# One of two scaled rows on VectorE, one chain sum on VectorE, and a list schedule that also waits for operations that are nearly late

## The chip, the core and the metric

The kernel runs on one core of a Trainium2 chip. The metric is the device time of one execution in microseconds (us), the median of several. The core's engines work side by side, each through its own queue in order: TensorE (PE) multiplies matrices, VectorE (DVE), ScalarE (ACT) and GpSimd (POOL) work on tiles in SBUF and PSUM, SyncE (SP) issues transfers, and POOL's queue issues some too.

## The reference

A decoder of two layers on 512 tokens of width 1024, in fp32. Layer 0 has a pooling mixer, layer 1 a gated spatial unit (SGU). Each layer is followed by an MLP of width 4096 with a squared ReLU, and both halves of a layer are modulated: the norm's output is scaled and shifted, and the branch is added through a gate, by vectors that come from a conditioning vector and a weight matrix ("ada").

```python
def rmsnorm(x, g):
    xf = x.astype(jnp.float32)
    y = xf * lax.rsqrt(jnp.mean(xf * xf, axis=-1, keepdims=True) + RMS_EPS)
    return (y * g.astype(jnp.float32)).astype(x.dtype)

def modulate(h, shift, scale):
    return h * (1.0 + scale[:, None, :]) + shift[:, None, :]
...
    z = jax.nn.gelu(h @ w_in, approximate=False)
    u, v = jnp.split(z, 2, axis=-1)
    v = layernorm(v, ln_g, ln_b)
```

What matters here is the end of layer 0's MLP: its result is added to x, each row of x is scaled by the power -1/2 of its mean square, and the scaled rows, transposed and modulated, are what the SGU's first matmul multiplies.

## The kernel before, in words

Every fp32 product is made of three matmuls on rounded parts: an operand is split into a high part that ACT writes (wh for weights, hb or as for activations, op for sums of operands) and a low part that DVE writes (wl, and hb, as, op again). So each weight tile costs ACT one conversion and DVE one subtraction of 128x1024.

The MLPs save matmuls with a scheme of seven products in place of eight: in the first GEMM (the "s" units, function s_prep for their weights and s_run for their matmuls) a unit's weight is one of four blocks b(r, n) of a quad, or a chain of sums and differences of them. The blocks live in the tiles tr, yr and raw. Sums are made by DVE (V.tensor_tensor) or by a transfer that adds to what stands in SBUF (function add: G.dma_start with accum_op, on POOL's queue). A unit's matmuls go into a PSUM buffer po, which ACT and DVE empty into g. The second GEMM (the "p" units) makes 24 matmuls of 512 columns a unit into pm; its results go through y into the residual x by the epilogue function gated, which also takes the sum of squares (on ACT, with the square written to tmp), and DVE makes sums of it.

Function rms calls for one power on POOL (rr<-sums,mhalf, a tile of 128x1) per tile of 128 tokens. Function scaled_rows(hf) makes the two tiles xs of half hf: X(t) times its rr, both by ACT. Function normed then has PE transpose xs in 16 blocks of 128x128 into px, and ACT and DVE modulate and split them (tt, hb). Function ending0 calls it for the first half of the tokens at the end of layer 0's MLP, ahead of the last of the pm matmuls, so that these hide the modulation. The SGU's matmuls follow (po at L102).

The order of the work inside an MLP is made by a planner, class Plan. It records the engine calls of mlp (a proxy in place of each engine) and replays them in an order of its own, and all instructions that it replays show as line L130, all others that go through the same wrapper as L102. PE's order is fixed. For each operation the planner has a cost (method cost: for DVE columns / 960 + 0.065 us, for ACT columns / 1200 + 0.095, for transfers a rate by size) and a due time late, counted back from the fixed stream of PE. It runs through time: when an engine is free it takes from the operations that are ready the one that is due first. Function yields, for DVE and ACT, lets the engine stand idle in favour of an operation that becomes ready soon:

```python
            for j in soon[e]:
                slack = late[j] - cost[j][1]
                if j != i and eta[j] < end and slack < end and late[i] - cost[i][1] > max(slack, eta[j]) + cost[j][0] and fits(j):
                    return True
```

Here i is the operation that it would start now, end the time at which i would be done by its cost, eta[j] the time at which j becomes ready, and slack the latest time at which j may start. So the engine waits only for a j that would be late if i went first. LEAD (layer 0) and LEAD1 (layer 1) hold the times at which the engines begin in the plan.

Of the kernel before, what the change touches and what calls it, by code (L numbers as in the profile page):

```python
# [9 lines left out]
AF = mybir.ActivationFunctionType  # L10
ALU = mybir.AluOpType
PSUM = bass.MemoryType.PSUM
PE = mybir.EngineType.PE
# [54 lines left out]
SPILL = (5, 7)  # L68

COLUMNS = (0, 5, 8, 10, 12, 14, 16, 17, 19, 21, 23, 24, 26, 28, 30, 31, 33, 35, 37, 38, 41, 44, 47, 50)  # L70
LEAD = dict(SP=0.0, POOL=0.0, ACT=9.0, DVE=9.0, PE=13.0, fresh=7.0)
LEAD1 = dict(SP=0.0, POOL=0.0, ACT=9.0, DVE=9.0, PE=10.0, fresh=7.0)
PLAN = (True, True)
A_PARTS = ((0, 0, 1, 2, 7), (2, 2, 2, 3, 4))

# [1 line left out]
class Plan:  # L77
# [125 lines left out]
    def run(self, lead):  # L203
# [5 lines left out]
        cost = [self.cost(o[0], o[1], o[3], o[4], o[5]) for o in ops]  # L209
# [25 lines left out]
        t, at = lead["PE"], {}  # L235
# [4 lines left out]
        late = [0.0] * N  # L240
        for i in range(N - 1, -1, -1):
            x = min([late[j] - cost[j][1] for j in succs[i] if j > i], default=t + 20)
# [15 lines left out]
        def fits(i):  # L258
            need = {}
            for x in self.tiles[i]:  # L260
                if x in place and x not in opened:
                    t, k = place[x]
                    if t in self.fresh and now < lead["fresh"] or k != nxt[t] + need.get(t, 0) or held[t] + need.get(t, 0) >= caps[t]:
                        return False
                    need[t] = need.get(t, 0) + 1
            return True

        unstarted = [len(p) for p in self.preds]
        eta = [0.0] * N
        soon = {e: set() for e in ready}  # L270

        def yields(e, i):

            end = now + cost[i][0]
            for j in soon[e]:
                slack = late[j] - cost[j][1]
                if j != i and eta[j] < end and slack < end and late[i] - cost[i][1] > max(slack, eta[j]) + cost[j][0] and fits(j):
                    return True
            return False

        events, now, free, queue = [], 0.0, {e: lead[e] for e in ready}, 0.0
        for x in lead.values():
            heapq.heappush(events, (x, -1))
        for i in range(N):
            if any(ap.space == PSUM and ap.tensor.name not in place for ap in ops[i][3] + ops[i][4]):
                when[i] = lead["PE"]
# [82 lines left out]
def decoder_kernel(ctx: ExitStack, tc: tile.TileContext, xtok, vecs, fgrow, ada0, ada1, pool_w, w1s, w1, w1f, w1b, w2, w_v, w_u, w_o, wsT, lnp, bs, out):  # L369
# [70 lines left out]
    def X(t):  # L440
        return x_[t // 2][:, t % 2]
# [163 lines left out]
    with (  # L605
# [58 lines left out]
        def rms(t):  # L664
            V.tensor_scalar(v0[:, t : t + 1], ss[:, t : t + 1], RMS_EPS, None, ALU.add)
            G.tensor_tensor(r0[:, t : t + 1], v0[:, t : t + 1], mhalf[:, 0:1], ALU.pow)
# [338 lines left out]
    def mlp(i, first, extra, last, ending):  # L1005
# [3 lines left out]
        with (  # L1009
# [102 lines left out]
            def s_prep(u):  # L1112
                c, j, m = u

                def b(r, n):
                    return blk(c, j, r, n)

                def add(o, r, n):
                    G.dma_start(o, w1b[quad_at(c, j), r, n], accum_op=ALU.add)


                t = b(0, 0)
                if m in (5, 6):
                    V.tensor_tensor(t, t, b(*CHAIN[m]), ALU.add)
                if m == 5:
                    add(b(0, 1), 1, 1)
                if m == 4 and (c, j) == (3, 1):
                    V.tensor_tensor(t, t, b(*CHAIN[4]), ALU.add)
                wb = b(1, 1) if m == 3 else b(1, 0) if m == 2 else b(0, 1) if m == 7 else t
                w = split(wb)  # L1130
                if m == 6 and (c, j) != (3, 1):
                    add(t, *CHAIN[4])

                nxt = (c, j + 1) if j == 0 else (c + 1, 0)
                more = {1: [(c, j, 0, 1), (c, j, 1, 1)], 5: [(*nxt, 0, 0)], 6: [(c, j, 1, 0)], 3: [(*nxt, 0, 1)], 7: [(*nxt, 1, 1)]}.get(m, [])
                for at in more:
                    if at[0] < 4:
                        blk(*at)
                return w
# [238 lines left out]
    def rms(t):  # L1378
        return power(sums.pop(t)[0][:, 3:4], 1)

    def scaled_rows(hf):
        xs = []
        for r in range(2):
            t = w4.tile([P, D], F32, name="xs", tag="w4")
            A.activation(t, X(2 * hf + r), AF.Copy, scale=rms(2 * hf + r))
            xs.append(t)
        return xs

    def normed(hf, i, n, xs=None, ks=range(0, KD, 2)):

        xs = xs or scaled_rows(hf)
        c = slice(256 * hf, 256 * hf + 256)
        for k in ks:
            px = bank("px")
            for q in range(2):
                for r in range(2):
                    T.transpose(px[:, 256 * q + P * r : 256 * q + P * r + P], xs[r][:, P * (k + q) : P * (k + q) + P], ident)
            tt = h32[0][:, k : k + 2, c] if h32 else sm.tile([P, 2, 256], F32, name="tt", tag="tmp")
            for q in range(2):
                a, b = scl[i][n][:, k + q : k + q + 1], mod(i, c_sh(n, k + q))  # L1400
                if q:
                    A.activation(tt[:, q], px[:, 256:512], AF.Identity, bias=b, scale=a)
                else:
                    V.tensor_scalar(tt[:, q], px[:, 0:256], a, b, ALU.mult, ALU.add)
            parts(H(slice(k, k + 2), c), tt)
# [25 lines left out]

    def ending0():
        h_[0] = hparts()
        normed(0, 1, 0)

# [253 lines left out]
```

## Time and profile before

| | us |
|---|---|
| runs of the kernel | 813.9, 812.17, 813.31 |
| median | 813.31 |
| the profiled execution | 813.07 |
| its span | 811.4 |
| PE busy in it | 789.8 (97%) |
| DVE busy | 671.5 (83%) |
| ACT busy | 502.8 (62%) |
| POOL busy | 86.5 (11%) |

The profile is of one execution. Its span runs from the first instruction to the last, and 1.7 us lie around it. A timeline row has the start, the duration, the engine, the line, the operation with out<-in by the program's names, the number of instructions in the row, and in brackets how long the engine stood idle before it and what ended that. A row of the waits has the waiting engine and tile, the engine and tile that it waited for, the total in us, the number of times and the longest. Neighbouring instructions of an engine overlap somewhat: a DVE operation of 1.22 us is followed by the next one after 1.13 us, and a matmul of 0.38 us by the next one after 0.22 us.

### The profile page before, as it was taken

Reading aid. Unit: us, or ns where it says so; the run is one execution under the profiler, and the core shown is the slowest. Engines: PE = TensorE matmul, PEld = TensorE weight load, DVE = VectorE, ACT = ScalarE, POOL = GpSimd, SP = SyncE. Lnnn points to the kernel's source line nnn. Section 1 sums busy time; section 2 is a strip of 40 time slices with the busy share of each in tenths; the row PEclk is TensorE's granted clock in tenths of the full one; section 3 lists DMA queues with packets and bytes.
Section 4 is the critical chain, followed back from the end, with each engine's and each line's share of the span. In section 5 each row is a group of like instructions: output and inputs, shape, how many; then the busy total and the mean of one; then the engine's idle time right before and its main releaser. Section 6 shows DMA issues by size and latency. Waiting matters only on the chain.

```text
span 811.4 us, 12430 instructions
## 1 busy us (share of the span) xinstructions
PE 789.8 (97%) x4796; PEld 714.0 (88%) x4796; DVE 671.5 (83%) x872; ACT 502.8 (62%) x718; POOL 86.5 (11%) x110
## 2 busy tenths in 40 slices
PE   5999999999999999989999999999999999999996
PEld 5778899999988888878889889989999998888885
DVE  5989788999779997986798976847787877998796
ACT  5486677767766665766333226757767676666672
POOL 4000000000011121030020001000000011112100
PEclk9999999999999999999999999999999999999999
DMA  8989878886999999126755655575777499999802
GB/s 343 417 306 317 332 223 280 270 269 185 345 272 229 258 226 277 47 79 249 269 174 189 217 173 207 185 232 145 219 235 199 140 362 253 207 227 204 224 1 104
DMA packets 46955, 184.40 MB, mean 227 GB/s; under 512 B 5272, under 2 KB 5424, under 8 KB 42672
## 3 DMA queue, kind: packets, MB, share of 16 engines
q1 hardware_dynamic: 36432, 129.33, 43.3%
q0 software_dynamic: 10032, 51.92, 30.6%
q10 hardware_dynamic: 432, 2.36, 0.7%
q8 instruction: 38, 0.62, 0.3%
q14 instruction: 21, 0.17, 0.1%
HBM read 177.28 MB, written 6.30 MB: 226 GB/s over the span
## 4 chain that ended last, share of the span: by engine, by line
PE 90%; DVE 3%; ACT 3%; DMA 2%; POOL 1%; issue 1%; SPq 0%; POOLq 0%; ACTq 0%; DVEq 0%
PE pm L130 33%; PE po L130 31%; PE po L102 22%; PE px L102 1%; DVE wl L130 1%; DMA x<-in_xtok 1%; PE pq L102 1%; DMA yr<-in_w1b 1%; POOL rr L130 1%; DVE op L130 1%; ACT wh L130 1%; DVE tmp L130 0%; PE pt L102 0%; DVE x L130 0%; SPq L102 0%
## 5 line engine op out<-in xcount | busy, mean ns | idle before, releaser
L130 PE MATMUL pm<-wh,op 128*128 128x512 f32 x896 | 268.3, 381 | 0.0
L130 PEld LDWEIGHTS pm<-wh,op 128*128 128x128 f32 x896 | 170.3, 190 | 24.1
L130 PE MATMUL po<-hb,wh 128*128 128x256 f32 (+1 forms) x976 | 181.8, 291 | 0.6 <-DVE hb L130 0.6
L130 PE MATMUL pm<-wl,op 128*128 128x512 f32 x448 | 170.4, 380 | 0.0
L130 PEld LDWEIGHTS po<-hb,wh 128*128 128x128 f32 x976 | 152.6, 192 | 4.8 <-DVE hb L130 1.0
L130 PE MATMUL po<-hb,wl 128*128 128x256 f32 (+1 forms) x489 | 139.7, 291 | 0.4 <-ACT hb L130 0.4
L130 ACT ACTIVATE op<-g 128x1024 fp32r<-128x1024 f32 x56 | 59.2, 1059 | 59.9 <-PE pm L130 53.0
L130 PEld LDWEIGHTS pm<-wl,op 128*128 128x128 f32 x448 | 85.1, 190 | 11.9
L130 PEld LDWEIGHTS po<-hb,wl 128*128 128x128 f32 x489 | 92.5, 192 | 2.6 <-ACT hb L130 0.6
L130 DVE TENSOR_TENSOR op<-g,op 128x1024 fp32r<-128x1024 f32 x56 | 68.4, 1223 | 26.2 <-ACT op L130 26.1
L130 PE MATMUL po<-as,wh 128*128 128x256 f32 x528 | 89.1, 275 | 0.0
L130 PEld LDWEIGHTS po<-as,wh 128*128 128x128 f32 x528 | 80.3, 192 | 0.0
L130 DVE TENSOR_TENSOR wl<-bt,wh 128x1024 fp32r<-128x1024 f32 x64 | 77.4, 1220 | 3.5 <-ACT wh L130 3.5
L130 ACT ACTIVATE wh<-bt 128x1024 fp32r<-128x1024 f32 x64 | 67.2, 1053 | 17.2 <-PE pm L130 13.7
L130 PE MATMUL po<-as,wl 128*128 128x256 f32 x264 | 72.8, 276 | 0.9 <-ACT g L130 0.9
L130 DVE TENSOR_TENSOR wl<-tr,wh 128x1024 fp32r<-128x1024 f32 x44 | 53.7, 1224 | 23.6 <-ACT wh L130 23.5
L102 PE MATMUL po<-hb,wh 128*128 128x512 f32 x240 | 71.6, 380 | 0.0
L130 ACT ACTIVATE g<-g 128x512 f32<-128x512 f32 x97 | 59.9, 633 | 16.6 <-DVE g L130 15.2
L130 ACT ACTIVATE wh<-tr 128x1024 fp32r<-128x1024 f32 x44 | 46.4, 1058 | 32.5 <-DVE tr L130 22.5
L102 DVE SCALAR_TENSOR_TENSOR ada<-ada,cb 128x1024 f32<-128x1024 f32 x42 | 50.9, 1221 | 6.3 <-DMA ada<-in_ada 6.1
L130 PEld LDWEIGHTS po<-as,wl 128*128 128x128 f32 x264 | 50.7, 192 | 1.1 <-ACT g L130 1.1
L102 PEld LDWEIGHTS po<-hb,wh 128*128 128x128 f32 x240 | 45.2, 189 | 6.7 <-DVE hb L102 0.6
(210 smaller groups left out, 1256.9 us busy)
## 6 DMA issues: line engine op xcount, KB each, us to landing
ada<-in_ada SPq DMA_DIRECT2D x76, 512.0 KB, 4.6
bt<-in_w POOLq DMA_DIRECT2D x24, 1024.0 KB, 10.4
yr<-in_w1b SPq DMA_DIRECT2D x22, 512.0 KB, 5.7
b<-in_w SPq DMA_DIRECT2D x20, 512.0 KB, 8.5
bt<-in_w SPq DMA_DIRECT2D x16, 512.0 KB, 7.7
tr<-in_w1b SPq DMA_DIRECT2D x11, 512.0 KB, 4.9
raw<-in_w1b SPq DMA_DIRECT2D x11, 512.0 KB, 5.0
yr<-in_w1b POOLq DMA_DIRECT2D x11, 512.0 KB, 5.4
```

Source lines behind the costliest of these rows:

```text
L102: return f(*a, **kw)
L130: self.ops.append((name, attr, lambda: f(*a, **kw), out, ins, kw))
```

## The change

Four things change. The planner's numbers get an entry wait (1.5 us for layer 0, 3.0 for layer 1), and yields takes a j whose latest start lies up to wait behind the end of i, so an engine also stands idle for an operation that would not yet be late. The events of the plan's clock are named one by one, so that the new entry is none of them. In s_prep, the sum b(0, 1) + b(1, 1) of the first quad of each layer is made by DVE in place of the adding transfer on POOL's queue. And scaled_rows can have the second of its two rows made by DVE (V.tensor_scalar), which ending0 asks for.

```diff
-LEAD = dict(SP=0.0, POOL=0.0, ACT=9.0, DVE=9.0, PE=13.0, fresh=7.0)
-LEAD1 = dict(SP=0.0, POOL=0.0, ACT=9.0, DVE=9.0, PE=10.0, fresh=7.0)
+LEAD = dict(SP=0.0, POOL=0.0, ACT=9.0, DVE=9.0, PE=13.0, fresh=7.0, wait=1.5)
+LEAD1 = dict(SP=0.0, POOL=0.0, ACT=9.0, DVE=9.0, PE=10.0, fresh=7.0, wait=3.0)
...
-                if j != i and eta[j] < end and slack < end and late[i] - cost[i][1] > max(slack, eta[j]) + cost[j][0] and fits(j):
+                if j != i and eta[j] < end and slack < end + lead["wait"] and late[i] - cost[i][1] > max(slack, eta[j]) + cost[j][0] and fits(j):
...
-        for x in lead.values():
-            heapq.heappush(events, (x, -1))
+        for e in (*ready, "fresh"):
+            heapq.heappush(events, (lead[e], -1))
...
-                if m == 5:
+                if m == 5 and (c, j) == first_quad:
+                    V.tensor_tensor(b(0, 1), b(0, 1), b(1, 1), ALU.add)
+                elif m == 5:
                     add(b(0, 1), 1, 1)
...
-    def scaled_rows(hf):
+    def scaled_rows(hf, on_v=False):
...
-            A.activation(t, X(2 * hf + r), AF.Copy, scale=rms(2 * hf + r))
+            if on_v and r:
+                V.tensor_scalar(t, X(2 * hf + r), rms(2 * hf + r), None, ALU.mult)
+            else:
+                A.activation(t, X(2 * hf + r), AF.Copy, scale=rms(2 * hf + r))
...
-        normed(0, 1, 0)
+        normed(0, 1, 0, scaled_rows(0, True))
```

PE's instructions and their order stay as they were. DVE has two rows more of the chain sums and one of the scaled row, ACT one row less, POOL's queue two adding transfers less. The planner's new order shows first at the end of layer 0's MLP. On DVE, behind the last weight remainder (wl) and the last of y (tmp and x1 are the epilogue of token tiles 2 and 3), the difference is:

```order
 L130 TENSOR_TENSOR wl_1299<-bt_1157,wh_1298 128x1024
 L130 TENSOR_TENSOR y_1163<-y_1163 128x512 x2
+L130 TENSOR_SCALAR xs_1307<-x0_1248,rr_1308 128x1024
 L130 TENSOR_TENSOR tmp_1276<-y_1163,gb_1208 128x512
 L130 TENSOR_TENSOR tmp_1278<-y_1163,gb_1208 128x512
```

The row with the plus is new: the second scaled row stands between y and the epilogue, and waits there for the second power. On ACT at the same place (wh the high part of the last weight tile, tmp the squares of the epilogue, rr_1306 and rr_1308 the two powers):

```order
-L130 ACTIVATE wh_1298<-bt_1157 128x1024
 L130 ACTIVATE tmp_1251,sums_1252<-x0_1248 128x512
 L130 ACTIVATE tmp_1259,sums_1252<-x0_1248 128x512
+L130 ACTIVATE wh_1298<-bt_1157 128x1024
 L130 ACTIVATE xs_1305<-x0_1248,rr_1306 128x1024
-L130 ACTIVATE xs_1307<-x0_1248,rr_1308 128x1024
 L130 ACTIVATE tmp_1276,sums_1277<-x1_1265 128x512
```

The last two squares come ahead of the weight conversion, and one of the two xs is gone.

The second place is ACT at the start of layer 0's MLP (yr, raw and tr hold blocks of weights, g takes the products from po). Before:

```order
L130 ACTIVATE wh_1011<-yr_997 128x1024
L130 ACTIVATE g_980<-po_993 128x2x256
L130 ACTIVATE g_980<-g_980 128x2x256
L130 ACTIVATE wh_1013<-raw_1006 128x1024
L130 ACTIVATE g_999<-po_1000 128x512
```

Now:

```order
L130 ACTIVATE wh_1011<-yr_997 128x1024
L130 ACTIVATE g_980<-po_993 128x2x256
L130 ACTIVATE g_980<-g_980 128x2x256
L130 ACTIVATE g_999<-po_1000 128x512
L130 ACTIVATE wh_1013<-raw_1006 128x1024
```

The emptying of po_1000 and the weight conversion have changed places. The third place is ACT at the start of layer 1's MLP (h32 are the normed rows, hb their high part, wh a weight conversion):

```order
 L130 ACTIVATE hb_4349<-h32_4352 128x2x256
 L130 ACTIVATE h32_4352<-px_4777,mods1_90,scl11_94 128x256
+L130 ACTIVATE hb_4349<-h32_4352 128x2x256
 L130 ACTIVATE wh_4781<-raw_4780 128x1024
-L130 ACTIVATE hb_4349<-h32_4352 128x2x256
```

The last hb moves ahead of the weight conversion. On DVE, next to it (hb the low part, ada here a tile that holds a sum of h32):

```order
 L130 TENSOR_SCALAR h32_4352<-px_4777,scl11_94,mods1_90 128x256
-L130 TENSOR_TENSOR hb_4351<-h32_4352,hb_4349 128x2x256
+L130 TENSOR_TENSOR hb_4351<-h32_4352,hb_4349 128x2x256 x2
 L130 TENSOR_TENSOR ada_4804<-h32_4352 128x1024
-L130 TENSOR_TENSOR hb_4351<-h32_4352,hb_4349 128x2x256
 L130 TENSOR_TENSOR h32_4352<-h32_4352 128x4x256
```

Both low parts stand ahead of that sum now.

## The prediction, on record before the changed kernel ran

> **What bounds the kernel now.** I read the page's engine totals first, then the chain, then PE's waits, then timelines at each wait. TensorE (PE) is the bound:
>
> ```profile
> PE 789.8 (97%) x4796; PEld 714.0 (88%) x4796; DVE 671.5 (83%) x872; ACT 502.8 (62%) x718; POOL 86.5 (11%) x110
> ```
>
> PE's instructions and their order are the same in both kernels, so the change can only win time in which PE stands, or lose some. The waits by engine, PE's own:
>
> ```profile
> core 0 of [0], span 811.4 us
> ...
> PE px L130 <- ACT xs L130: 2.9, 2, 2.2
> PE po L130 <- ACT g L130: 0.9, 1, 0.9
> PE po L130 <- DVE hb L130: 0.6, 2, 0.3
> ...
> PE po L130 <- ACT hb L130: 0.4, 1, 0.4
> ```
>
> These four belong to three places, which I call A (end of layer 0's MLP, 352 us), B (start of layer 0's MLP, 123 us) and C (start of layer 1's MLP, 514 to 516 us). The rows left out lie at the program's start or inside the mixers (L102), which the planner doesn't order. The four add up to 4.8 us of waiting, and to somewhat more of lost time, as the places show.
>
> **Place A, the transition.** PE's timeline: the last down-projection matmuls (pm), the 16 transposes (px) of the scaled rows xs, 24 more pm held back to cover the norm, and the SGU's po.
>
> ```profile
> 352.36 0.38 PE L130 MATMUL pm<-wh,op 128*128 128x512 f32 x1
> 354.93 0.33 PE L130 MATMUL px<-ident,xs 128*128 128x128 f32 x1 [2.19 <-ACT xs L130]
> 355.97 2.33 PE L130 MATMUL px<-ident,xs 128*128 128x128 f32 x15 [0.71 <-ACT xs L130]
> 357.96 0.78 PE L130 MATMUL pm<-wh,op 128*128 128x512 f32 x1
> ...
> 364.31 0.38 PE L130 MATMUL pm<-wh,op 128*128 128x512 f32 x1
> 364.53 0.38 PE L102 MATMUL po<-wh,hb 128*128 128x512 f32 x1
> ```
>
> Dense matmuls of 512 columns follow each other after 0.22 us (364.31 to 364.53), so the first px could have started at 352.58. It started at 354.93, and the second at 355.97. Behind the stall the clock halves for one stretch (the windows view; the first column after the engines is the granted clock):
>
> ```profile
> 357.20:360.60 3.40, 3.40 (x12) 2.92 (x11) 3.05 (x5) 3.37 (x7) 0.00 (x0) 0.50 0.41 133
> ```
>
> That stretch holds 12 matmuls in place of 15 (3.40 / 0.22). Without a stall, 16 transposes take what they take elsewhere, with no slow matmul behind them:
>
> ```profile
> 508.24 1.91 PE L130 MATMUL px<-ident,xs 128*128 128x128 f32 x16
> ```
>
> So po would start at 352.58 + 1.91 + 24 x 0.22 = 359.77 and not at 364.53: **4.76 us** to win (1.91 includes the last one's latency, so the figure is on the low side).
>
> What PE waited for is the two xs on ACT, and these for the two powers rr on POOL:
>
> ```profile
> L130 POOL TENSOR_TENSOR rr<-sums,mhalf x2: 543/2872/5200, 348.5 to 353.7; 128x1 f32<-128x1 f32 x2
> ```
>
> ```profile
> 353.73 2.19 ACT L130 ACTIVATE xs<-x,rr 128x1024 f32<-128x1024 f32 x2 [5.75 <-POOL rr L130]
> ```
>
> The first power took 5.20 us, the second 0.54, on the same 128x1 tile. In the meantime DVE ran seven operations with two operands in SBUF without a gap:
>
> ```profile
> 348.20 0.33 DVE L130 TENSOR_SCALAR sums<-sums 128x1 f32<-128x1 f32 x2
> 348.44 1.22 DVE L130 TENSOR_TENSOR wl<-bt,wh 128x1024 fp32r<-128x1024 f32 x1
> 349.57 1.29 DVE L130 TENSOR_TENSOR y<-y 128x512 f32<-128x512 f32 x2
> ...
> 351.98 1.29 DVE L130 TENSOR_TENSOR x<-x,tmp 128x512 f32<-128x512 f32 x2
> ```
>
> The first power ended at 348.49 + 5.20 = 353.69, that is 0.42 us after this row's end (353.27). Two other powers of the trace, and what DVE ran beside the second of them:
>
> ```profile
> 488.42 0.56 POOL L102 TENSOR_TENSOR rr<-sums,mhalf 128x1 f32<-128x1 f32 x1 [59.98 <-DVE sums L102]
> ```
>
> ```profile
> 801.19 0.86 POOL L130 TENSOR_TENSOR rr<-sums,mhalf 128x1 f32<-128x1 f32 x1 [21.61 <-DVE sums L130]
> ```
>
> ```profile
> 800.97 0.68 DVE L130 TENSOR_TENSOR x<-x,cb 128x512 f32<-128x512 f32 x1
> ```
>
> The first, with no such work on DVE, took 0.56. The second took 0.86 and ended at 802.05, 0.40 us after that one two-operand operation (801.65). My reading: POOL was kept out until DVE's unbroken run of two-operand work ended. The Trainium skill (SBUF — State Buffer, section "SBUF: two separate sides") says that such a DVE operation and a GpSimd operation that reads SBUF exclude each other for one whole instruction, and that the blocked one goes on some 115 ns after DVE's end. By that letter the power would have come free behind the wl of 348.44, before 350; the trace has 353.69, so here the exclusion lasted over the run, or its length has another cause (the first rival).
>
> **What the change does at A.** The second xs goes to DVE, behind y and ahead of the four operations that followed (the pieces of the order stand with the change). DVE works in order, so it now stops at xs_1307 until both powers are done, and tmp and x1 queue behind it. Who waits for those: the norm of tiles 2 and 3, whose transposes come long after the first. On ACT, the squares come ahead of one weight conversion, and ACT has one xs less. Replayed from before's times: sums at 348.20, wl 348.44, y to 350.86; DVE stops; first power free at 350.86 + 0.42 = 351.28, second at 351.82. xs on ACT, half of the row's 2.19 with overlap (1.14): 351.31 to 352.45. xs on DVE by the nearest one-operand scaling of this shape:
>
> ```profile
> L102 DVE TENSOR_SCALAR v<-v,ag,rr 128x1024 f32<-128x1024 f32 x4 | 3.2, 811 | 0.6 <-POOL rr L102 0.4
> ```
>
> 0.81 us: 351.85 to 352.66, against 352.58 where PE wants it. That alone closes the gap to 0.1. And sums come earlier: an ada product that stood here moves ahead of DVE's idle times nearer 300 us,
>
> ```profile
> 319.89 1.22 DVE L130 SCALAR_TENSOR_TENSOR ada<-ada,cb 128x1024 f32<-128x1024 f32 x1
> ```
>
> which takes 1.13 us (1.22 less the overlap of neighbours) out of the stretch before sums. Cover: about 1 us. I take the whole 4.76; if the cover fails, each 0.1 us of lateness costs 0.1.
>
> **Place B.** ACT (first fence) and PE (second):
>
> ```profile
> 120.37 1.06 ACT L130 ACTIVATE wh<-yr 128x1024 fp32r<-128x1024 f32 x1 [0.64 <-DMA yr<-in_w1b]
> ...
> 122.49 1.04 ACT L130 ACTIVATE wh<-raw 128x1024 fp32r<-128x1024 f32 x1
> 123.43 0.58 ACT L130 ACTIVATE g<-po 128x512 f32<-128x512 f32 x1
> ```
>
> ```profile
> 122.66 0.28 PE L130 MATMUL po<-as,wl 128*128 128x256 f32 x1
> 122.77 0.39 PE L130 MATMUL po<-as,wh 128*128 128x256 f32 x2
> 124.06 0.38 PE L130 MATMUL po<-as,wl 128*128 128x256 f32 x1 [0.91 <-ACT g L130]
> ```
>
> PE's next matmul was due at 122.77 + 2 x 0.11 = 122.99 (0.11 from the first two rows) and started at 124.06: 1.07 lost. It needed the PSUM buffer that g<-po empties, and ACT did wh<-raw first, itself late since wh<-yr had waited 0.64 for the accumulating DMA. In the new order the two have changed places. Now g_999<-po_1000 starts where wh_1013 stood, by 122.49 at the latest, and by 121.9 with the DMA's 0.64 gone; its 0.58 ends between 122.5 and 123.1. **1.07 us** won (0.95 at least). Added for it: the chain sum on DVE, one two-operand operation of 128x1024 per layer, 1.22 us by the wl row above. It takes the place of one accumulating transfer on POOL's queue. DVE has 6.9 of 32 us free there, and 2.7 of 36 in the stage behind, where it has least room (the third column of times is DVE's):
>
> ```profile
> 92.00:124.00 32.00, 31.16 (x168) 27.77 (x167) 25.10 (x25) 25.73 (x39) 1.95 (x2) 1.00 0.75 244
> 124.00:160.00 36.00, 35.94 (x321) 35.94 (x322) 33.33 (x42) 25.11 (x36) 3.45 (x4) 1.00 0.86 281
> ```
>
> So 1.22 fits, and I cost it at nothing; in the stage behind it would still fit, and what doesn't fit would be PE's to wait, up to 1.2 in each layer.
>
> **Place C.** ACT, DVE, PE:
>
> ```profile
> 514.13 1.06 ACT L130 ACTIVATE wh<-raw 128x1024 fp32r<-128x1024 f32 x1
> 515.08 0.62 ACT L130 ACTIVATE hb<-h 128x512 fp32r<-128x512 f32 x1
> ```
>
> ```profile
> 514.42 1.22 DVE L130 TENSOR_TENSOR ada<-h 128x1024 f32<-128x1024 f32 x1
> 515.73 0.69 DVE L130 TENSOR_TENSOR hb<-h,hb 128x512 fp32r<-128x512 f32 x1
> ```
>
> ```profile
> 515.75 0.38 PE L130 MATMUL po<-hb,wl 128*128 128x256 f32 x1 [0.37 <-ACT hb L130]
> 516.48 0.49 PE L130 MATMUL po<-hb,wh 128*128 128x256 f32 x2 [0.35 <-DVE hb L130]
> ```
>
> The last hb stood behind wh on ACT, and its remainder behind ada on DVE. In the new order hb_4349 stands ahead of wh_4781 on ACT, and DVE's likewise has both hb_4351 ahead of ada_4804. hb moves from 515.08 to 514.13, the remainder from 515.73 to 514.78, PE's second start from 516.48 to 515.53: **0.95 us** won. What moves back is wh, by 0.6 us, and ada, by 0.7; nothing on PE waits for either in the waits above, and 0.7 is less than one conversion (1.06) of lead.
>
> **Elsewhere.** The waiting rule reorders DVE and ACT in both MLPs. Where PE is dense already it can win nothing. The end of the program:
>
> ```profile
> 803.81 0.69 DVE L130 TENSOR_TENSOR tmp<-pm,gb 128x512 f32<-128x512 f32 x1 [2.16 <-PE pm L130]
> ```
>
> DVE idles 2.16 us for PE's last pm; the new order puts two more epilogue operations (0.69 each) into that idle time: nothing, 0 to 0.6 at worst.
>
> **Sum.** The profiled execution took 813.07 us (span 811.4 and 1.7 around it), 0.24 under the median of 813.31. 813.07 - 4.76 - 1.07 - 0.95 = 806.29, so **806.3**. 0.2% is 1.6 us, about what a measurement can tell.
>
> **Rivals.**
> 1. *The 5.2 us belong to POOL, not to DVE's run.* Then the first power ends 5.2 after sums wherever DVE stands: with sums 1.13 earlier 352.56, the second 353.10, xs on DVE 353.9, and px 15 starts some 2.0 earlier than now; the halved clock (about 1.4) may go or stay. A gives 2.0 to 3.4, the total 807.6 to 809.0. For it: of the powers shown only this one is long. Against it: 0.56 at 488.42 after 59.98 us of idleness, and the 0.42 that matches the 0.40 of 801.19. The Trainium skill (GPSIMD Engine Reference, section "Instruction dispatch") has a first call of newly loaded code cost about 6 us, which would be such a case; the 488.42 row speaks against it. Chance 0.15.
> 2. *The gap moves to the start of the SGU.* Its first hb, its weights' remainders and their loads must follow po, now 4.76 us earlier. Replayed with before's durations they have 1 to 2 us of room, but the transfers' share of that is the least sure. If it is too short, 1 to 2.5 comes back: 807.3 to 808.8. Chance 0.12.
> 3. *Slower: DVE falls behind in layer 0's first GEMM.* Waiting leaves DVE idle on purpose, in the stage where 2.67 of 36 us are free (and 1.22 of new work stands ahead of it). From more than 2.67 per 36 us of waiting on, PE waits once a unit: at 0.25 in each of 35 units 8.75 us go, more than the 6.78 won: about 815. The order shows urgent work moved forward there, not late. Chance 0.06.
> 4. *It doesn't do what it says:* the planner's times aren't the chip's, and the three stalls stay in other places: 812 to 813.5. Chance 0.04.
>
> The forecast has 0.63. Range: 805.0 (0.28 if the first hb wait of C goes too, 0.2 for transposes that overlap their successors, 0.24 for run against run, and the rest of 1.3 for waits that I don't see) to 809.0 (rivals 1 and 2 in). Faster by over 0.2%: 0.63 + 0.15 + 0.12 = 0.90; within: 0.04; slower: 0.06.
>
> **What would show it.** Right: no PE wait for xs, clock 1.00 about 357, first power under 3 us and ended 0.4 after DVE's y; PE's wait for g and for ACT's hb gone; a remaining hb wait by DVE. Wrong: a power of 5 us with DVE idle (rival 1), a new wait of po at L102 behind the transition (rival 2), PE waits for wl in 124 to 160 (rival 3).

## The result and the profile after

| | before | changed |
|---|---|---|
| median, us | 813.31 (812.17 to 815.63, 7 runs) | 808.27 (807.09 to 811.49, 7 runs) |
| ratio | 1 | 0.9947, 95% interval 0.9929 to 0.9965 |
| the profiled execution, us | 813.07 (span 811.4) | 811.49 (span 809.8) |

The change makes the kernel faster by 0.35 to 0.71%, that is 2.8 to 5.8 us. The time lies in the range, and 2 us above the 806.3 that was named, which is below the fastest of the seven runs. The profiled execution of the changed kernel is the slowest of the seven, which turned out to matter.

PE's waits in the changed kernel, those at the start of the program and the shortest left out:

```profile
PE po L130 <- DVE g L130: 1.7, 4, 0.6
PE pm L130 <- DVE wl L130: 0.8, 1, 0.8
PE po L102 <- ACT hb L102: 0.5, 1, 0.5
PE po L130 <- DVE hb L130: 0.5, 2, 0.3
PE pm L130 <- DVE op L130: 0.5, 1, 0.5
```

The waits for xs, for ACT's g and for ACT's hb at L130 are gone, at A, B and C as foreseen (the wait for hb at L102, in the SGU, stood in the kernel before too). Three rows are new: g by DVE, wl and op.

**Place A.** PE's timeline over the transition, then the powers, DVE, and the clock of the stretch that had 0.50:

```profile
353.43 0.38 PE L130 MATMUL pm<-wh,op 128*128 128x512 f32 x1
353.64 1.91 PE L130 MATMUL px<-ident,xs 128*128 128x128 f32 x16
355.31 0.46 PE L130 MATMUL pm<-wh,op 128*128 128x512 f32 x1
...
360.57 0.38 PE L102 MATMUL po<-wh,hb 128*128 128x512 f32 x1
```

```profile
L130 POOL TENSOR_TENSOR rr<-sums,mhalf x2: 543/1666/2789, 347.8 to 350.5; 128x1 f32<-128x1 f32 x2
```

```profile
347.73 1.22 DVE L130 TENSOR_TENSOR wl<-bt,wh 128x1024 fp32r<-128x1024 f32 x1
348.86 1.29 DVE L130 TENSOR_TENSOR y<-y 128x512 f32<-128x512 f32 x2
351.12 0.75 DVE L130 TENSOR_SCALAR xs<-x,rr 128x1024 f32<-128x1024 f32 x1 [0.98 <-POOL rr L130]
```

```profile
357.20:360.60 3.40, 3.40 (x18) 2.97 (x17) 2.84 (x7) 3.30 (x7) 0.55 (x1) 1.00 0.98 377
```

From the last pm ahead of the transposes to the SGU's first po there were 12.17 us (352.36 to 364.53); now there are 7.14 (353.43 to 360.57). The first power ends at 350.56, 0.41 us after y (350.15). DVE idles 0.98 and then scales; xs is done at 351.87, 1.8 us before PE wants it.

**The new waits.** One of the four for g. ACT, DVE and PE about 150 us:

```profile
147.17 2.01 ACT L130 ACTIVATE wh<-tr 128x1024 fp32r<-128x1024 f32 x2 [2.14 <-DMA tr<-in_w1b]
```

```profile
148.26 2.36 DVE L130 TENSOR_TENSOR wl<-tr,wh 128x1024 fp32r<-128x1024 f32 x2 [2.66 <-ACT wh L130]
150.54 0.68 DVE L130 TENSOR_TENSOR g<-po,g 128x512 f32<-128x512 f32 x1
...
152.27 0.68 DVE L130 TENSOR_TENSOR g<-g,po 128x512 f32<-128x512 f32 x1
```

```profile
153.00 0.38 PE L130 MATMUL po<-hb,wl 128*128 128x256 f32 x1 [0.58 <-DVE g L130]
```

To be read from the top: ACT stood 2.14 us for the adding transfer tr, DVE 2.66 for ACT's wh, two remainders wl and then g queued behind that, and PE needed the PSUM buffer that g empties. DVE had been idle, so it isn't short of time there; it stood in front of one late transfer, in order. Added up over the nine places of the new waits (152, 172, 191, 229, 651, 660, 663 twice and 672 us), from one matmul's start to the next less the dense spacing, PE loses 4.8 us. Of the 6.9 us won at A, B and C (5.0, 1.07, 0.8) these leave 2.1, and the two profiled executions differ by 1.6.

### The profile page after: what moved, and what is told of

The parts are those of the page before. It is cut to its first block, busy times and chain, and to the rows that moved or that the text cites. A ratio compares the mean times of both kernels' runs of the same rounds, so it can differ in the third digit from the quotient of the medians.

```text
span 809.8 us, 12414 instructions
## 1 busy us (share of the span) xinstructions
PE 789.7 (98%) x4796; PEld 712.0 (88%) x4796; DVE 672.7 (83%) x875; ACT 502.1 (62%) x717; POOL 84.0 (10%) x108
## 4 chain that ended last, share of the span: by engine, by line
PE 69%; DMA 12%; DVE 10%; issue 4%; ACT 3%; SPq 0%; POOL 0%; POOLq 0%; DVEq 0%; ACTq 0%
PE pm L130 32%; PE po L102 17%; PE po L130 17%; DVE wl L130 3%; DMA b<-in_w 2%; DMA bt<-in_w 2%; DMA tr<-in_w1b 2%; DMA raw<-in_w 2%; DMA ada<-in_ada 2%; DVE ada L102 1%; PE px L102 1%; DMA x<-in_xtok 1%; ACT wh L130 1%; PE pq L102 1%; DVE g L130 1%
## 5 line engine op out<-in xcount | busy, mean ns | idle before, releaser
L130 PE MATMUL pm<-wh,op 128*128 128x512 f32 x896 | 268.2, 380 | 0.7 <-DVE op L130 0.5
L130 PEld LDWEIGHTS pm<-wh,op 128*128 128x128 f32 x896 | 169.3, 189 | 26.2 <-DVE op L130 1.9
L130 PE MATMUL po<-hb,wh 128*128 128x256 f32 (+1 forms) x976 | 182.0, 291 | 0.5 <-DVE hb L130 0.5
L130 PE MATMUL pm<-wl,op 128*128 128x512 f32 x448 | 169.9, 379 | 0.8 <-DVE wl L130 0.8
L130 PEld LDWEIGHTS po<-hb,wh 128*128 128x128 f32 x976 | 152.4, 192 | 4.7 <-DVE hb L130 0.8
L130 PE MATMUL po<-hb,wl 128*128 128x256 f32 (+1 forms) x489 | 139.8, 291 | 1.7 <-DVE g L130 1.7
L130 PEld LDWEIGHTS po<-hb,wl 128*128 128x128 f32 x489 | 92.4, 191 | 4.4 <-DVE g L130 2.5
L130 PEld LDWEIGHTS pm<-wl,op 128*128 128x128 f32 x448 | 84.7, 189 | 13.0 <-DVE wl L130 1.2
L130 ACT ACTIVATE op<-g 128x1024 fp32r<-128x1024 f32 x56 | 59.2, 1058 | 53.6 <-PE pm L130 45.7
L130 DVE TENSOR_TENSOR op<-g,op 128x1024 fp32r<-128x1024 f32 x56 | 68.5, 1223 | 25.0 <-ACT op L130 24.9
L130 PE MATMUL po<-as,wh 128*128 128x256 f32 x528 | 89.0, 275 | 0.0
L130 PEld LDWEIGHTS po<-as,wh 128*128 128x128 f32 x528 | 80.2, 192 | 0.0
L130 DVE TENSOR_TENSOR wl<-bt,wh 128x1024 fp32r<-128x1024 f32 x64 | 77.3, 1220 | 2.6 <-ACT wh L130 2.6
L130 ACT ACTIVATE wh<-bt 128x1024 fp32r<-128x1024 f32 x64 | 67.1, 1052 | 19.4 <-PE pm L130 15.0
L130 ACT ACTIVATE g<-g 128x512 f32<-128x512 f32 x97 | 59.6, 631 | 28.0 <-DVE g L130 26.8
L130 DVE TENSOR_TENSOR wl<-tr,wh 128x1024 fp32r<-128x1024 f32 x44 | 53.4, 1223 | 26.5 <-ACT wh L130 26.5
L130 PE MATMUL po<-as,wl 128*128 128x256 f32 x264 | 72.6, 275 | 0.0
L102 PE MATMUL po<-hb,wh 128*128 128x512 f32 x240 | 71.6, 380 | 0.0
L130 ACT ACTIVATE wh<-tr 128x1024 fp32r<-128x1024 f32 x44 | 46.0, 1056 | 18.6 <-DVE tr L130 9.4
L102 DVE SCALAR_TENSOR_TENSOR ada<-ada,cb 128x1024 f32<-128x1024 f32 x42 | 50.8, 1220 | 5.9 <-DMA ada<-in_ada 5.8
L102 PEld LDWEIGHTS po<-hb,wh 128*128 128x128 f32 x240 | 45.1, 189 | 6.8 <-DVE hb L102 0.6
L130 PEld LDWEIGHTS po<-as,wl 128*128 128x128 f32 x264 | 50.7, 192 | 0.0
```

The costliest lines, as they stand in the source:

```text
L102: return f(*a, **kw)
L130: self.ops.append((name, attr, lambda: f(*a, **kw), out, ins, kw))
```

## The experiments

The theory after the first look: A, B and C are won whole, and what is missing goes to transfers that land late, because the new plan orders them otherwise; how late differs from one execution to the next. The rivals: the new order itself makes those waits; DVE's added work and idling make them; the length of the power is POOL's own.

**The changed kernel once more (e1_again).** No edit.

> The changed kernel once more, unaltered, for a second profile. In its first profile PE lost about 4.8 us at nine new waits (four of po for DVE's g, three of pm for op, one for wl, one for ACT's wh), each behind a load that landed late. Theory: these come from transfers that collide, so their sum differs from one execution to the next; the second profile loses 1 to 4 us in such waits, and the median is 807 to 809.5. Rival (the order alone makes them): the same nine waits, 4.8 us within 0.5. Place A, B and C stay won in either case: no wait for xs or for ACT's g.

Measured: 807.8 us (805.67 to 810.49), ratio 0.9946 (0.9926 to 0.9966). The profiled execution took 805.67, the fastest of its six, and its PE waits from 18 us on are these:

```profile
PE po L102 <- ACT hb L102: 0.5, 1, 0.5
PE po L130 <- DVE hb L130: 0.5, 2, 0.3
PE po L102 <- DVE hb L102: 0.3, 1, 0.3
```

None of the nine. Program and order are the same, so the order alone doesn't make them. The adding transfers tr of 125 to 195 us in the kernel before, in the changed one's first profile and in this one (size, median us to landing):

```profile
tr<-in_w1b POOLq DMA_DIRECT2D x3, 512.0 KB, 5.6
```

```profile
tr<-in_w1b POOLq DMA_DIRECT2D x3, 512.0 KB, 7.8
```

```profile
tr<-in_w1b POOLq DMA_DIRECT2D x3, 512.0 KB, 7.3
```

The one of 138 us took 8.7 in the first profile and 7.3 in the second. In both, tr lands later than before, and in the execution of 811.49 it crosses the point where PE waits. The two yr on SP's queue right behind that tr took 8.0 and 7.8 in the one and 6.6 and 6.5 in the other, while POOL needed 0.85 us to issue tr in both: all the loads of that stretch were slower, not the adding transfer alone. Likewise the two b of 646 and 643 us took 13.2 and 10.3 (median of the two). The expectation of 1 to 4 us in a second profile was still too high: it was 0.

**Scaled row and chain sums, no waiting rule (e2_rows_chain).**

```diff
-LEAD = dict(..., wait=1.5)
-LEAD1 = dict(..., wait=3.0)
+LEAD = dict(..., wait=0.0)
+LEAD1 = dict(..., wait=0.0)
```

> The changed kernel with both entries wait at 0: only the scaled row and the chain sums are on DVE. Theory: place A is won whole (5.0 us), place B by the 0.64 us that ACT no longer waits for the adding transfer, place C stays lost (1.15), and none of the new waits of 124 to 230 and 645 to 672 us comes, since the loads keep their order: 807.7 (807 to 808.5), with less spread than the changed kernel. Rival (the new waits come from DVE's added work): the waits of po for DVE's g stay, 1.5 us or more in the profile, 809 to 811.

Measured: 809.88 us (808.48 to 811.77), ratio 0.9969 (0.9956 to 0.9982). A is won, C is lost as foreseen, but behind B waits stand that I had not expected (1.2 and 1.5 us lost at 126 and 143). ACT, then PE, at the first:

```profile
125.31 1.06 ACT L130 ACTIVATE wh<-tr 128x1024 fp32r<-128x1024 f32 x1 [2.43 <-DMA tr<-in_w1b]
126.28 0.58 ACT L130 ACTIVATE g<-po 128x512 f32<-128x512 f32 x1
```

```profile
126.91 0.38 PE L130 MATMUL po<-as,wl 128*128 128x256 f32 x1 [1.03 <-ACT g L130]
```

So ACT no longer waits for yr, and waits for tr a little later, again with g queued behind. The rival's number fits better than mine, but its mechanism doesn't: these two waits are ACT's, for a transfer (only a third one, 0.5 at 193 us, is for DVE's g). The three tr from 125 to 195 us took 7.6 us here (median), with no waiting rule.

**The scaled row alone (e3_rows_alone).**

```diff
+            if on_v and r:
+                V.tensor_scalar(t, X(2 * hf + r), rms(2 * hf + r), None, ALU.mult)
...
+        normed(0, 1, 0, scaled_rows(0, True))
```

> The kernel before with one edit, the second scaled row on DVE; no waiting rule, no chain sum on DVE. Theory: the first power ends 0.4 us after the end of DVE's y and PE doesn't wait for xs: 5.0 us won, B and C as before (1.07 and 1.15 lost): 808.3 (807.5 to 809). Rival 1 of the prediction (the 5.2 us belong to POOL): already against the changed kernel's profile, 2.79; here it would be 5.2 again and 811 or more. Second rival (A needs the squares that the waiting rule moves forward): a px wait of 0.1 to 1.3 us, 808.5 to 809.6.

Measured: 808.49 us (808.07 to 809.3), ratio 0.9950 (0.9937 to 0.9964), no wait for xs, power 2.79. One edit of the four gives the measured gain. The SGU's start gives some of A back here (0.15, 0.24 and 0.77 lost at 361 to 371 us, where the kernel before lost 0.38), for example:

```profile
372.31 0.48 PE L102 MATMUL po<-wh,hb 128*128 128x512 f32 x1 [0.72 <-DVE hb L102]
```

That is rival 2 of the prediction at a small price; with the waiting rule in layer 0 it is back to 0.38. C is lost here (1.15) as foreseen, and 0.97 for DVE's g at 652 us; at B nothing is lost, though the order there is that of before. Against e2_rows_chain only the chain sums are left out: the median is 1.4 us lower (the two intervals just overlap), and tr took 5.8.

**The waiting rule alone (e4_wait_alone).**

```diff
-    normed(0, 1, 0, scaled_rows(0, True))
+    normed(0, 1, 0)
...
-    if m == 5 and (c, j) == first_quad:
+    if m == 5 and False:
```

> The kernel before with the waiting rule alone (1.5 and 3.0); both scaled rows on ACT, chain sums by transfers. Theory: A stays (the first power runs until DVE's run of two-operand work ends, 4 us or more, px waits 2 to 3 us), B and C are won (1.07 and about 0.8), and the new waits cost 1 to 5 us: 812 to 816, no faster than before. Rival (the rule is worth its 1.9 and costs nothing by itself): 811.4.

Measured: 811.02 us (809.54 to 813.45), ratio 0.9988 (0.9974 to 1.0001): no difference that shows. But A went otherwise than expected. The powers, and DVE beside them:

```profile
L130 POOL TENSOR_TENSOR rr<-sums,mhalf x2: 934/2604/4273, 347.6 to 348.5; 128x1 f32<-128x1 f32 x2
```

```profile
347.40 0.68 DVE L130 TENSOR_TENSOR y<-y 128x512 f32<-128x512 f32 x1
347.99 0.21 DVE L130 TENSOR_SCALAR sums<-sums 128x1 f32<-128x1 f32 x1
...
351.06 1.28 DVE L130 TENSOR_TENSOR x<-x,tmp 128x512 f32<-128x512 f32 x2
```

The rule put one y between the two sums. The first power ended with that y (348.08 + 0.41 = 348.49), the second took 4.27 and ended 0.43 after x (352.34). So PE loses only 0.4 at px (the wait of 0.3 for the second xs), and the transition takes 7.65 us. The gain is lost elsewhere:

```profile
PE po L130 <- DVE g L130: 2.0, 2, 1.5
PE po L102 <- DVE wl L102: 1.1, 1, 1.1
PE po L102 <- ACT wh L102: 0.8, 1, 0.8
```

**Light ada transfers in the changed kernel (e5_light_after) and in the kernel before (e6_light_before).**

```diff
+        if attr == "dma_start" and out[0].tensor.name.startswith("ada"):
+            self.ops.append((name, attr, lambda: f(a[0][:, 0:64], a[1][:, 0:64], **kw), out, ins, kw))
...
```

and their products read the 64 columns fifteen times. The replay line is L138 in these.

> The changed kernel with the planner's order untouched, but the 42 or so ada transfers inside the two MLPs bring 64 columns in place of 1024 (their products read these over and over, so the modulation vectors of the later parts are not the reference's). About 16 MB fewer are moved. Theory: the new waits of PE come from transfers that land late because ada's share the 16 DMA engines with them; the adding transfer tr lands within 6.5 us instead of 6.8 to 8.7, PE waits for DVE's g nowhere in layer 0, and the median is 805 to 806.3 with runs within 2 us. Rival (the order itself, or DVE idling on purpose, makes them): 807 to 808.5 as in the changed kernel, and waits for g in the profile.

> The kernel before with the same ada transfers cut to 64 columns (the same part of the result left out), the control for the kernel above. Theory: before has few waits behind late transfers, at most place B (1.07) and nothing in the other stages: 811 to 812.3, so that changed against before is worth 6 us or more when ada's traffic is gone. Rival (the traffic costs both kernels alike): 2 us less as well, 810.

Measured: 807.49 (806.99 to 809.07), ratio 0.9940 (0.9924 to 0.9957), and 811.89 (809.88 to 814.93), ratio 0.9996 (0.9983 to 1.001). PE's waits in the changed kernel with light transfers, and its tr:

```profile
PE pm L138 <- DVE wl L138: 0.8, 1, 0.8
PE po L138 <- DVE g L138: 0.6, 1, 0.6
```

```profile
tr<-in_w1b POOLq DMA_DIRECT2D x3, 512.0 KB, 5.6
```

From 125 us on tr lands as in the kernel before, and no new wait is left in layer 0; the one for g stands at 648 us, those for op and wl at 657 to 670, in layer 1 (2.7 us lost), with ada's transfers as light there. So in this profile, with ada's transfers light, tr isn't late. That this is what freed PE in layer 0 isn't shown, since e1_again lost nothing there with full transfers. The median didn't fall for it, and the difference to the control, 4.4 us of medians, is no larger than with full transfers. My theory's number (805 to 806.3) failed.

The control shows something of A. Its waits for xs are those of the kernel before (2.34 and 0.92 us lost at px, 2.35 and 0.92 there), but the granted clock stayed whole behind them:

```profile
351.60 0.38 PE L138 MATMUL pm<-wh,op 128*128 128x512 f32 x1
354.15 0.33 PE L138 MATMUL px<-ident,xs 128*128 128x128 f32 x1 [2.18 <-ACT xs L138]
...
362.07 0.38 PE L102 MATMUL po<-wh,hb 128*128 128x512 f32 x1
```

```profile
356.40:359.80 3.40, 3.40 (x20) 3.05 (x19) 3.05 (x5) 3.37 (x7) 0.00 (x0) 1.00 0.51 135
```

The transition took 10.47 us, 3.3 more than in the changed kernel. Of the 12.17 in the kernel before, 1.7 belong to the halved clock, which didn't follow on the same stall here.

**Without the chain sums (e7_rows_wait), and with the rule in layer 1 alone, without them (e8_rows_w1).**

```diff
-                if m == 5 and (c, j) == first_quad:
-                    V.tensor_tensor(b(0, 1), b(0, 1), b(1, 1), ALU.add)
-                elif m == 5:
+                if m == 5:
...
-LEAD = dict(..., wait=1.5)
+LEAD = dict(..., wait=0.0)
```

(the last two lines in e8_rows_w1 only).

> The changed kernel without the chain sums on DVE (adding transfers as before): scaled row and waiting rule. Theory: the sum on DVE is worth nothing once g stands ahead of the weight conversion at B; 807 to 808.5, B without a wait of PE. Rival (the sum costs, as the scaled row alone at 808.49 against scaled row with sums at 809.88 suggests): 806 to 806.9. Second rival (B's gain comes from the sum): 808.5 to 809 with PE waiting at 122 us.

> Scaled row on DVE and the waiting rule in layer 1 alone (0 and 3.0), no chain sums on DVE. Theory: layer 0 keeps the order and the landings of the scaled row alone (808.49, tr within 6 us), place C is won (0.8), and layer 1's loads at 645 to 672 us may land late (0 to 2.8): 807.5 to 809. Rival (layer 0's rule is what wins, at the SGU's start 0.8 and at B): 808.5 to 809.5. Were it under 807, layer 0's rule would cost more than it wins.

Measured: 809.48 (807.69 to 811.89), ratio 0.9962 (0.9947 to 0.9976), and 809.1 (807.58 to 810.84), ratio 0.9956 (0.9937 to 0.9974). Neither differs from the changed kernel by more than the intervals. In the first, B has no wait though yr comes by transfer, as the order of g and wh would have it; PE loses 1.1 at 209 and 1.0 at 650 us for g. Its tr of 138 us has the neighbours that it has in the changed kernel and landed in 5.8 us, the next two in 7.5 and 7.6. In the second B is lost again (1.2).

**A stop of DVE without the scaling (e9_stop).** The kernel before, both xs on ACT:

```diff
+            q = rms(2 * hf + r)
+            if on_v and r:
+                q, p = sm.tile([P, 1], F32, name="rq", tag="rq"), q
+                V.tensor_scalar(q, p, 1.0, None, ALU.mult)
+            A.activation(t, X(2 * hf + r), AF.Copy, scale=q)
...
+        normed(0, 1, 0, scaled_rows(0, True))
```

> The kernel before, both scaled rows still on ACT, but the second one's power goes through a DVE copy of 128x1 behind y, so DVE stops there for the powers as it does in the changed kernel, and no 128x1024 work moves. Theory (the power runs until DVE's unbroken run of two-operand work ends): first power about 2.8 us in place of 5.2, xs end one after the other about 353.5, PE stands about 0.9 us in place of 3.2 and its clock stays whole: 3 to 4 us won, 808.5 to 810. Rival (what helps is the scaling moved off ACT, and the power's length is its own): power 5.2, 811.5 to 813.

Measured: 808.07 (807.42 to 810.1), ratio 0.9952 (0.9938 to 0.9966). DVE, POOL and PE:

```profile
348.85 1.28 DVE L130 TENSOR_TENSOR y<-y 128x512 f32<-128x512 f32 x2
351.12 0.15 DVE L130 TENSOR_SCALAR rq<-rr 128x1 f32<-128x1 f32 x1 [0.98 <-POOL rr L130]
```

```profile
L130 POOL TENSOR_TENSOR rr<-sums,mhalf x2: 544/1668/2792, 347.8 to 350.5; 128x1 f32<-128x1 f32 x2
```

```profile
352.83 1.86 PE L130 MATMUL px<-ident,xs 128*128 128x128 f32 x15 [0.70 <-ACT xs L130]
```

This decides the cause at A. An operation of 0.15 us, which only makes DVE stand for 0.98 us, shortens the power from 5.20 to 2.79 us as the scaled row does, and gives a gain as large as the change's (0.9952 against 0.9947). The second scaling on ACT leaves a wait of 0.70 at px, which moving it saves: the transition takes 8.06 us here and 7.14 in the changed kernel.

**A plan with slower transfers (e10_slow_plan), and the rule in layer 0 alone (e11_w0).**

```diff
-            return (5.05 * mb, 3.6 + 4.8 * mb) if kw.get("accum_op") else (2.7 * mb, 0.9 + 5.2 * mb)
+            return (5.9 * mb, 4.6 + 5.6 * mb) if kw.get("accum_op") else (3.1 * mb, 1.5 + 6.0 * mb)
```

and, in the second, wait=0.0 in LEAD1.

> The changed kernel, and the planner takes transfers to be slower: 3.1 us per MB and 1.5 + 6.0 per MB to landing (2.7, 0.9 + 5.2 before), adding ones 5.9 and 4.6 + 5.6 (5.05, 3.6 + 4.8). Theory: PE's new waits come from transfers that land later than the plan has them, so a plan with later landings loads urgent weights ahead of ada and loses less: 805.7 to 807.2, fewer and shorter waits for g, op and wl in the profile. Rival (the stretch at 640 to 665 us is short of bandwidth whatever the order): 807.5 to 808.5 with waits at 648 to 672.

> The changed kernel with the waiting rule in layer 0 alone (1.5 and 0). Theory: C is lost again (0.8), the waits of 657 to 672 us (up to 1.9 in two of three profiles of this order) go, what is left in layer 0 stays: 807 to 808.8, no difference that these runs can tell from the changed kernel. Rival (layer 1's rule costs more than it wins): under 806.8; second rival (it wins): over 809.

Measured: 841.01 (840.23 to 842.05), ratio 1.0355 (1.0339 to 1.0372), and 807.82 (806.8 to 809.96), ratio 0.9947 (0.993 to 0.9964). The slower plan is 28 us slower than the kernel before and 33 slower than the changed one. The longest piece of the chain before the transition, and PE's longest waits:

```profile
358.64 3.81 DMA gb<-gain
```

```profile
PE px L130 <- ACT xs L130: 9.4, 1, 9.4
PE pm L130 <- DVE wl L130: 7.5, 4, 2.3
PE pm L130 <- ACT wh L130: 6.3, 3, 2.1
```

It also moves the transfer of the gain vector (gb) and the ada products to the end of the MLP, where the epilogue waits for them. So a plan that takes transfers to be slower isn't a safer one here, against the theory. The rule in layer 0 alone is no different from the changed kernel; its profile has waits at 190 to 228 us (1.6) and C's (1.15) but none at 650 to 672.

**The rule only where it moves no transfer (e12_parts).**

```diff
-... slack < end + lead["wait"] and ...
+... slack < end + (lead["wait"] if lead["PE"] > 11 and now > 150 or lead["PE"] < 11 and now < 40 else 0.0) and ...
```

without the chain sums.

> The scaled row on DVE, and the waiting rule only where it moves no transfer: in layer 0 from the plan's 150th us on, in layer 1 up to its 40th. The chain sums are by transfers, SP's order is that of the kernel before. DVE now stops for the powers right behind wl, with one y moved ahead and one behind the stop. Theory of the power (it runs until DVE's run of two-operand work ends): first power ends 0.4 us after that wl, so it takes 1.4 to 1.7 us, against 2.79 with two y between and 5.20 without a stop. Theory of the transfers: A and C won (5.0 and 0.8), the SGU's start as in the changed kernel, and no more waits behind late transfers than the kernel before has (up to 1): 806.5 to 807.8. Rival (the order of the transfers doesn't matter): as the scaled row alone less C, and waits for g, op and wl as in the changed kernel: 807.8 to 808.5.

Measured: 808.23 (806.65 to 808.98), ratio 0.9941 (0.9926 to 0.9957). The transfers' part of the theory isn't borne out: B is lost again (1.07), the SGU's start too (1.2), g at 650 (0.96), and the sum is that of the scaled row alone. The power's part is. Only the wl stands beside it now:

```profile
348.72 1.21 DVE L130 TENSOR_TENSOR wl<-bt,wh 128x1024 fp32r<-128x1024 f32 x1
350.90 0.75 DVE L130 TENSOR_SCALAR xs<-x,rr 128x1024 f32<-128x1024 f32 x1 [0.98 <-POOL rr L130]
```

```profile
L130 POOL TENSOR_TENSOR rr<-sums,mhalf x2: 544/1066/1588, 348.8 to 350.3; 128x1 f32<-128x1 f32 x2
```

1.59 us, ended 0.42 after that wl (349.93 to 350.35). Of the twelve, no version is faster than the changed kernel by more than the runs can tell.

**Late transfers over all profiles.** The slower plan left out (and the runs named by their first letters), the profiles fall into two groups in each layer. In layer 0 it is the median of the three tr from 125 to 195 us, in layer 1 the median of the two b from 643 to 651 us, each from issue to landing:

| | profiles | us to landing |
|---|---|---|
| tr, layer 0's early order as before | before, e3, e6, e8, e9, e12 | 5.6 to 6.3 |
| tr, with the rule in layer 0, the chain sums, or both | after, e1, e2, e4, e7, e11 | 7.2 to 7.8 |
| tr, with both and light ada transfers | e5 | 5.6 |
| b, no rule in layer 1, or only up to its 40th us | before, e2, e3, e6, e9, e11, e12 | 6.7 to 8.8 |
| b, with the rule in layer 1 | after, e1, e4, e5, e7, e8 | 10.3 to 13.2 |

So the later landings come with the edits, in every profile with full transfers, and chain sums alone bring them in layer 0 too. What PE loses by them differs: in layer 0, behind B, 2.0, 0, 1.65, 1.1 and 1.6 us with the rule (after, e1, e4, e7, e11), 3.2 with the chain sums alone (e2), and nothing with the early order as before (before, e3, e8, e9, e12); in layer 1, from 640 to 680 us, 2.75, 0, 0.9, 1.3 and 0.75 with the rule (after, e1, e4, e7, e8) and 0, 0, 0.97, 0, 0 and 0.96 without (before, e2, e3, e9, e11, e12). With the rule and without, the means are 1.3 against 0 and 1.1 against 0.3. By this estimate of mine the late transfers cost 1.3 + 0.8 = 2.1 us in the mean, about what the median lies above the sum; with five or six profiles each and sums from 0 to 2.75 it is a rough one.

## Why the prediction held, and where it was too high

- *Place A* was right in mechanism, and in size for this pair of profiles: 4.76 us expected, 12.17 - 7.14 = 5.03 measured, clock 1.00, the power ended 0.41 after y. Of these 1.7 are the clock, which stayed whole in e6_light_before at the same stall; the prediction took the halved stretch of one profile as given, and how many executions have it isn't known. The cover was 1.8 us where about 1 was expected. That the stop and not the scaling brings it is shown by e9_stop; the prediction put the two together.
- *Place B*, 1.07, was right for this pair of profiles and too high as a typical value. The six profiles with before's order of g and wh at B and with yr by transfer lose 1.07, 1.21 and 1.07 (before, e8_rows_w1, e12_parts) and nothing in the other three (e3_rows_alone, e6_light_before, e9_stop): 0.56 on average. All six profiles with the new order there (after, e1, e4, e5, e7, e11) lose nothing at B. The chain sum on DVE was costed at nothing; with the rule on no run shows it to be worth or to cost anything, without the rule it comes with a later tr and a median 1.4 us higher (e2_rows_chain against e3_rows_alone).
- *Place C*, 0.95 expected, 0.81 measured (0.54 and 0.62 lost before, 0.34 after): ACT's hb comes as expected, and DVE's remainder still ends 0.18 after PE wants it.
- *The step that failed* is "Where PE is dense already it can win nothing", with nothing subtracted for what it can lose there. The rule and the chain sums also moved transfers (ada's and yr's about tr, b's and bt's at 640 to 653 us), which the prediction didn't cost. In their new places they land later (7.2 to 7.8 in place of 5.6 to 6.3 for tr, 10.3 to 13.2 in place of 6.7 to 8.8 for b), and what PE loses by it differs between executions: 0 us in one profile, 4.8 in the other. The first of these, 805.67, the fastest of all runs of the changed kernel, is where the sum of the measured gains lies (813.07 - 6.9 = 806.2); the median is 2 us above it.
- *Luck* has a part in the range. Its upper end, 809.0, was set for rivals 1 and 2, and neither happened; the median lies where they were priced. The range's 0.24 for run against run was small too: the seven runs of the changed kernel spread over 4.4 us. What tells the forecast from these rivals is the profile (the power, the clock, the waits), not the time.
- *Rival 1* (the 5.2 us are POOL's own) fell with 2.79, and with 1.59 in e12_parts. *Rival 2* doesn't occur in the changed kernel (0.38 lost at 373 us, as in the kernel before at 377); with the scaled row and no early rule in layer 0 it does, with 0.8 more (e3_rows_alone, e12_parts), in e9_stop it doesn't. *Rival 3* had the right engine and a wrong reason: PE does wait for DVE in layer 0, but DVE idles for late weights there, not for want of time. *Rival 4* fell.
- What stays open: why the same transfers land 1 to 3 us later in one execution than in the next, and what in the new order makes them late: the neighbours of tr don't settle it (5.8 in e7_rows_wait), and light ada transfers help tr but not b. How the 2 us above the sum divide between the layers is an estimate, since profiles with the old order have such waits too (0.94 at 653 us in e6_light_before), and the runs can't tell differences of 1 us between versions.

## What to carry to other kernels

When a 128x1 operation on POOL takes microseconds, look at what DVE runs beside it before moving work: a stop of DVE of 1 us was worth 4 here. When a scheduler's rule changes, compare the transfer queues' order as well as the compute engines', and cost every transfer that changes neighbours; a profile with a dense PE says nothing on how near to late its loads are. Take a second profile of the same kernel before explaining the waits of the first.

## What the runs showed of the hardware

At the transition the power's length goes by DVE's unbroken run of operations with two operands in SBUF: 0.93 us beside one of 512 columns (e4_wait_alone), 1.59 beside one of 1024 (e12_parts), 2.79 beside three operations, 4.27 and 5.20 beside six and seven, each ended 0.41 to 0.43 us after the run, and 0.54 with DVE stopped. In the kernel before, DVE went on without a gap behind the seven, with an operation that has one operand in PSUM (tmp<-pm,gb at 353.18 us), and the power came free there too. The Trainium skill (SBUF — State Buffer, section "SBUF: two separate sides") has the exclusion last for one whole instruction; here it lasted over runs of up to seven. One power of the SGU is against a simple rule: it got through between two such operations that follow without a gap, 0.42 us after the first (so in the kernel before, and it took the same 1.40 us in the changed one and in e9_stop).

```profile
404.80 1.21 DVE L102 TENSOR_TENSOR wl<-ur,wh 128x1024 fp32r<-128x1024 f32 x1
405.94 1.22 DVE L102 TENSOR_TENSOR v<-v,lnt 128x1024 f32<-128x1024 f32 x1
```

```profile
405.03 1.40 POOL L102 TENSOR_TENSOR rr<-rv,mhalf 128x1 f32<-128x1 f32 x1 [2.34 <-DVE rv L102]
```

What sets the two cases apart was not tried.
